# Two-layer attention and expert kernel on one core: window attention of two tiles ahead of the last tile's keys and values, and 120 instead of 40 expert gathers carried from layer 0 into layer 1

## The chip, the cores and the metric

The kernel runs on one core of a Trainium2 chip. The metric is the device time of one execution in microseconds (us). A run is the whole program: both layers, from the loading of the inputs to the stored output.

## What is computed

Two layers over 512 latent tokens and 256 context tokens, width 1024, all in float32. The latent tokens are four tiles of 128 tokens (lat 0 to lat 3), the context is two (ctx 0, ctx 1). Cut to what matters:

```
for l in range(2):
    p  = modulate(h, ...) @ w_in                      # queries, keys, values, lat and ctx
    o1 = softmax(q_mla . [kc_mla, k_mla]) v           # every latent query reads all 256 + 512 keys
    o2 = softmax([q_swa . kc_swa, q_swa . k_near, sink]) v   # 256 context keys + tokens within 128
    h  = h + g1 * (concat(o1, o2) @ w_out)
    b  = modulate(h, ...)
    s  = (b @ wq) . sub_keys                          # 8 heads, two halves of 128 keys
    idx, g = the 16 best experts of 16384 per head    # 128 experts per token
    h  = h + g2 * sum_k g[k] * gelu(b . u[idx[k]]) * v[idx[k]]
```

The context gets its attention and expert step in layer 0 alone. The tile numbers matter: the window attention `o2` of lat 0 reads the keys of lat 0 and 1, that of lat 1 those of lat 0 to 2. The all-key attention `o1` of every tile reads the keys of all four.

## The kernel before

The expert step is done in two ways. **Sparse tiles** (in layer 0 ctx 0, ctx 1 and lat 3; in layer 1 lat 0 and lat 1) fetch the rows that were chosen: the generator `experts` (line 742) yields once per gather, 128 gathers of `u` rows and then 128 of `v` rows for each tile. One gather moves 128 rows of 4 KB into one of five `gv` buffers (line 754, issued by POOL), and VectorE (DVE) does a dot product with it (line 758) or adds it to `vacc` (line 768), four gathers later. After a tile's last gather its new `h` is written to memory (lines 771 to 775). **Dense tiles** (layer 0: lat 0 to 2; layer 1: lat 2 and 3) go through all 16384 experts in `dense_experts` (line 857) as 128 steps: SyncE (SP) loads 512 KB of `uT` and 512 KB of `v`, ScalarE (ACT) and DVE split them into two parts (lines 867, 868), TensorE (PE) multiplies (`A`, line 921; `o`, line 894), and every 16 steps two loads bring the gate weights `G` (line 909).

A layer is first attention and routing, then the dense phase. In the attention part the steps are Python generators run one after the other by `run(...)` or interleaved by `par(...)`: `KV` projects keys and values, `Q` queries, `A` is the attention of one tile (line 524), first the all-key heads, then the window heads, `O` is the output projection, `R` or `RF` routing, `G` and `GH` the choice of the experts and, for a dense tile, the one-hot gate matrices. This gives the order of priority. The instructions themselves are placed by a scheduler that simulates engine times at build time, within dependencies and buffers; each engine then executes its own queue strictly in order. In the dense phase the order is written out by hand (`manual_schedule`).

The gathers of a layer are dealt out in three portions at the end of the layer's code. In layer 0 there are 3 x 256 = 768: 353 (`AHEAD` 0.46) stand ahead of the dense phase, `rest` = 768 - 353 - 40 = 375 are spread over the 128 dense steps, 2.93 to a step, and 40 (`SPILL`) are left over. These 40 are the generator `left`, run in layer 1 after `Q(t, 0)`. They belong to lat 3, whose `h` is complete only behind them, so the keys and values of lat 3 in layer 1 come after them. In layer 1 there are 512: 368 ahead of its dense phase, 144 spread over it from step 16 on. Line 1076 holds the order at the start of layer 1:

```python
run(KV(c, 0, 1), KV(t, 0, 1), Q(t, 0), left, KV(t, 2, 3), A(t, 0), O((t, 0)))
run(RF(t, 0), Q(t, 1), A(t, 1))
run(G(t, 0), O((t, 1)), Q(t, 2, 3))
```

The weights of each projection pass through four `w4` buffers on SP's queue, and three buffers (`fm_tile`) hold the transposed inputs and the attention outputs.

Of the kernel before, what the change touches and what calls it, by code (L numbers as in the profile page):

```python
# [64 lines left out]

LATE = (0, 16)

SPILL = (40, 0)

AHEAD = (0.46, 0.72)  # L70

# [18 lines left out]
def body(ctx: ExitStack, tc: tile.TileContext, I, out):  # L90
# [275 lines left out]
    def fm_tile(name):  # L366
        return att.tile([P, KC, P], F32, tag="aT", name=name, bufs=3)
# [143 lines left out]
    def over_sums(o, su):  # L511


        rs = sm.tile([P, H], F32, tag="rsu", name="rsu")
        nc.vector.reciprocal(rs, su)
        pr = m1()
        for c in range(H // 2):
            for x in range(2):
                nc.tensor.matmul(pr[x * VD:(x + 1) * VD, c * P:(c + 1) * P],
                                 rs[:, 2 * c + x:2 * c + x + 1].to_broadcast([P, VD]), ident, start=True, stop=True)  # L520
        ov = o.rearrange("p c t -> p (c t)")
        nc.vector.tensor_tensor(ov, ov, pr, OP.mult)

    def attend(l, st, i, qT, sqT, K, kv):

        nk = C if st == "ctx" else C + S
        oT = fm_tile("oT")
        su = sm.tile([P, H], F32, tag="su", name="su")
        for c in range(H // 2):
            yield  # L530
            pe = []
            for h in (2 * c, 2 * c + 1):
                ps = big()
                for k0 in range(0, nk, 512):
                    n = min(512, nk - k0)
                    nc.tensor.matmul(ps[:, k0:k0 + n], qT[:, h, :], kv["kT"][:, h, k0:k0 + n],  # L536
                                     start=True, stop=True)
                pe.append(soft(ps, nk, su[:, h:h + 1], None))
            pair_pv(pe, nk, lambda x, kt: kv["v"][:, kt, (2 * c + x) * VD:(2 * c + x + 1) * VD],
                    oT[:, c, :])  # L540
        over_sums(oT[:, 0:4, :], su)
        su = sm.tile([P, H], F32, tag="su", name="su")
        j0, j1 = (0, 0) if st == "ctx" else (max(0, i - 1), min(NT[st], i + 2))
        nk2 = C + (j1 - j0) * P
        for c in range(H // 2):
            yield
            g = c // 2
            pe = []
            for x in range(2):
                hp = x * SD  # L550
                q = sqT[hp:hp + SD, c, :]
                ps = big()
                nc.tensor.matmul(ps[:, :C], q, kv["skT"][hp:hp + SD, g, :C], start=True, stop=True)
                for j in range(j0, j1):
                    dst = ps[:, C + (j - j0) * P:C + (j - j0 + 1) * P]
                    nc.tensor.matmul(dst, q, kv["skT"][hp:hp + SD, g, C + j * P:C + (j + 1) * P],
                                     start=True, stop=(j == i))
                    if j != i:
                        nc.tensor.matmul(dst, identb, mlo if j < i else mhi, start=False, stop=True)
                h = 2 * c + x  # L560
                pe.append(soft(ps, nk2, su[:, h:h + 1], K["nsink"][:, h:h + 1]))
            pair_pv(pe, nk2, lambda x, kt: kv["sv"][:, kt if kt < 2 else kt + j0, g * SD:(g + 1) * SD],
                    oT[:, 4 + c, :])
        over_sums(oT[:, 4:8, :], su)
        return oT

    def out_proj(l, tiles, oT, m):

# [410 lines left out]
    def run(*gens):  # L979
        for g in gens:  # L980
            for _ in g:
                pass
# [11 lines left out]
    for l in range(L):  # L994
# [3 lines left out]
        with ExitStack() as es:  # L998
# [4 lines left out]
            K = layer_consts(l)  # L1003
            kv = {"kT": att.tile([QK, H, C + S], F32, tag="kT", name="kT"),
                  "v": att.tile([P, (C + S) // P, H * VD], F32, tag="v", name="v"),
                  "skT": att.tile([P, 2, C + S], F32, tag="skT", name="skT"),
                  "sv": att.tile([P, (C + S) // P, 2 * SD], F32, tag="sv", name="sv")}
            qs, os, bs = {}, {}, {}

            def KV(st, *tiles):  # L1010
                aT = norms(l, st, tiles, m, st == "lat")
                yield
                yield from project_kv(l, st, tiles, aT, K, kv)

            def Q(st, *tiles):
                aT = norms(l, st, tiles, m, False)
                yield
                yield from project_q(l, st, tiles, aT, K, qs)

            def KVQ(st, *tiles):  # L1020
# [2 lines left out]
                yield from project_kv(l, st, tiles, aT, K, kv)  # L1023
                yield from project_q(l, st, tiles, aT, K, qs)

            def A(st, i):
                os[st, i] = yield from attend(l, st, i, *qs.pop((st, i)), K, kv)

            def O(*tiles):
                res = yield from out_proj(l, tiles, [os.pop(x) for x in tiles], m)  # L1030
                bs.update(zip(tiles, res))
# [7 lines left out]
            def RF(st, i):  # L1039

                bT, bd = bs.pop((st, i))
                half = chosen("")

                def mid(res):
                    yield from choose(*res[0], *half, 0, H // 2)

                r, = yield from route(l, [bT], mid)
                got[st, i] = r, bd, half
# [8 lines left out]
            c, t = "ctx", "lat"  # L1057
            if l == 0:
                a = ada(l, m)
                next(a)  # L1060
                run(KVQ(c, 0, 1))
                run(a, A(c, 0), O((c, 0)))
                early = qs[c, 1][1][:, 0, 0:1]
                par((A(c, 1), 16), (R((c, 0)), 16))
                run(G(c, 0), ada(1, mods[1], early))
                run(KV(t, 0, 1), KV(t, 2, 3), Q(t, 0, 1), A(t, 0), O((c, 1), (t, 0)))
                par((A(t, 1), 8), (R((c, 1), (t, 0)), 24))
                run(G(c, 1), O((t, 1)), Q(t, 2, 3))
                par((A(t, 2), 8), (R((t, 1)), 24), (GH(0), 48))
                run(O((t, 2)))  # L1070
                par((A(t, 3), 8), (R((t, 2)), 24), (GH(1), 48))
                run(O((t, 3)))
                par((R((t, 3)), 24), (GH(2, True), 48))
                run(G(t, 3))
            else:
                run(KV(c, 0, 1), KV(t, 0, 1), Q(t, 0), left, KV(t, 2, 3), A(t, 0), O((t, 0)))
                run(RF(t, 0), Q(t, 1), A(t, 1))
                run(G(t, 0), O((t, 1)), Q(t, 2, 3))
                par((A(t, 2), 8), (R((t, 1)), 24))
                run(G(t, 1), O((t, 2)))  # L1080
                par((A(t, 3), 8), (R((t, 2)), 24))
                run(O((t, 3)))
                par((R((t, 3)), 24), (GH(2), 48))
                run(GH(3, True))
        with ExitStack() as es:
# [9 lines left out]
            free[0] = False  # L1095
            rest = n - int(n * AHEAD[l]) - SPILL[l]
            for e, _ in enumerate(dense):
# [4 lines left out]
            left = rows  # L1102
# [57 lines left out]
```

## Time and profile before

| | us |
|---|---|
| time, median of 3 runs | 4489.13 (4487.55 to 4492.19) |
| the profiled execution, its own time | 4481.78 |
| its span from first to last instruction | 4480.0 |
| PE busy | 3617.1 (81%) |
| DVE busy | 3352.5 (75%) |
| ACT busy | 1687.4 (38%) |
| POOL busy | 1629.0 (36%) |
| mean granted TensorE clock | 0.894 of full speed |

The profiled execution lies 7.35 us below the median. Its stages, by the first and last matmuls of each: attention and routing of layer 0 to 1401 us, dense phase of layer 0 from there to 2517 us, attention and routing of layer 1 to 3640 us, dense phase of layer 1 to the end. All times inside a run are microseconds from the start of the span.

### The profile page before, as it was taken

Reading aid. Unit: us, or ns where it says so; the run is one execution under the profiler, and the core shown is the slowest. Engines: PE = TensorE matmul, PEld = TensorE weight load, DVE = VectorE, ACT = ScalarE, POOL = GpSimd, SP = SyncE. Lnnn points to the kernel's source line nnn. Section 1 sums busy time; section 2 is a strip of 40 time slices with the busy share of each in tenths; the row PEclk is TensorE's granted clock in tenths of the full one; section 3 lists DMA queues with packets and bytes.
Section 4 is the critical chain, followed back from the end, with each engine's and each line's share of the span. In section 5 each row is a group of like instructions: output and inputs, shape, how many; then the busy total and the mean of one; then the engine's idle time right before and its main releaser. Section 6 shows DMA issues by size and latency. Waiting matters only on the chain.

```text
span 4480.0 us, 58044 instructions
## 1 busy us (share of the span) xinstructions
PE 3617.1 (81%) x19934; PEld 2907.9 (65%) x19934; DVE 3352.5 (75%) x7566; ACT 1687.4 (38%) x3244; POOL 1629.0 (36%) x1402
## 2 busy tenths in 40 slices
PE   6885778477887999999999668676676468999997
PEld 2453357256776898888988545444455467888886
DVE  1247778989678788777877832778989977777777
ACT  1342231155575333333333234232224653444443
POOL 2016565544101444444444510255443443222222
PEclk8997788788997999999999889898888579999999
DMA  8588898888666999999999952789899789889897
GB/s 303 171 284 305 307 346 310 299 300 311 219 204 229 327 318 315 325 334 328 332 311 318 330 175 92 258 320 336 310 335 345 260 307 337 301 298 304 298 316 245
DMA packets 467481, 1306.48 MB, mean 292 GB/s; under 512 B 41568, under 2 KB 147808, under 8 KB 467184
## 3 DMA queue, kind: packets, MB, share of 16 engines
q0 software_dynamic: 199744, 726.26, 46.0%
q1 hardware_dynamic: 267440, 576.50, 37.0%
q8 instruction: 157, 2.57, 0.2%
q14 instruction: 140, 1.15, 0.1%
HBM read 1240.70 MB, written 61.90 MB: 291 GB/s over the span
## 4 chain that ended last, share of the span: by engine, by line
PE 24%; issue 24%; DVE 23%; DMA 13%; ACT 8%; POOL 7%; SPq 0%; POOLq 0%; ACTq 0%; DVEq 0%
DVE vacc L768 8%; POOL gv L754 7%; PE m L644 5%; DVE v L868 4%; ACT u L867 3%; DMA gv<-v,idx 3%; DVE gv L758 2%; DMA gv<-u,idx 2%; PE m L372 2%; DMA raw<-uT 2%; PE acc L852 2%; PE A L921 2%; DMA w<-w_in 2%; PE o L894 2%; PE m L507 1%
## 5 line engine op out<-in xcount | busy, mean ns | idle before, releaser
L754 POOL DMA_INDIRECT gv<-v,idx x640 | 782.1, 1222 | 1143.4 <-DVE vacc L768 807.3
L754 POOL DMA_INDIRECT gv<-u,idx x640 | 784.6, 1226 | 964.3 <-DVE a L758 635.4
L894 PE MATMUL o<-v,W 128*128 128x512 f32 x3840 | 943.0, 398 | 71.3 <-ACT W L867 71.0
L921 PE MATMUL A<-b,u 128*128 128x384 f32 (+1 forms) x6144 | 962.5, 313 | 41.6 <-ACT w L924 29.8
L921 PEld LDWEIGHTS A<-b,u 128*128 128x128 f32 x6144 | 936.3, 192 | 70.8 <-ACT w L924 39.3
L894 PEld LDWEIGHTS o<-v,W 128*128 128x128 f32 x3840 | 719.0, 191 | 228.9 <-ACT W L867 84.6
L768 DVE SCALAR_TENSOR_TENSOR vacc<-gv,a,vacc 128x1024 f32<-128x1024 f32 x635 | 811.2, 1277 | 55.7 <-DMA gv<-v,idx 48.5
L758 DVE CUSTOM_DVE_ANT_0 gv<-gv,btok 128x1024 f32<-128x1024 f32 x640 | 768.0, 1218 | 98.0 <-DMA gv<-u,idx 97.1
L867 ACT ACTIVATE W<-w 128x384 fp32r<-128x384 f32 (+1 forms) x256 | 120.7, 472 | 1042.5 <-DVE w L927 1042.5
L868 DVE TENSOR_TENSOR u<-raw,u 128x1024 fp32r<-128x1024 f32 x256 | 313.5, 1224 | 166.3 <-ACT u L867 164.1
L372 PE MATMUL m<-w,aT 128*128 128x256 f32 (+3 forms) x704 | 259.7, 518 | 86.7 <-DMA w<-w_in 51.4
L644 PE MATMUL m<-bT,wq 128*128 128x128 f32 x2560 | 313.7, 279 | 5.0 <-DMA wq<-wq 4.1
L868 DVE TENSOR_TENSOR v<-raw,v 128x1024 fp32r<-128x1024 f32 x256 | 311.9, 1218 | 3.6 <-ACT v L867 3.5
L644 PEld LDWEIGHTS m<-bT,wq 128*128 128x128 f32 x2560 | 301.1, 195 | 10.7 <-DMA wq<-wq 5.7
L867 ACT ACTIVATE u<-raw 128x1024 fp32r<-128x1024 f32 x256 | 267.7, 1046 | 62.5 <-DMA raw<-uT 62.5
L867 ACT ACTIVATE v<-raw 128x1024 fp32r<-128x1024 f32 x256 | 267.4, 1044 | 4.6 <-PE o L894 4.5
L372 PEld LDWEIGHTS m<-w,aT 128*128 128x128 f32 x704 | 142.7, 213 | 190.5 <-DMA w<-w_in 69.2
L868 DVE TENSOR_TENSOR W<-w,W 128x384 fp32r<-128x384 f32 (+1 forms) x256 | 125.7, 491 | 144.7 <-ACT W L867 144.6
L927 DVE TENSOR_TENSOR w<-w,G 128x192 f32<-128x192 f32 (+1 forms) x512 | 143.6, 319 | 68.4 <-DMA G<-Gd 55.2
L852 PE MATMUL acc<-o,o 128*128 128x128 f32 x768 | 140.0, 337 | 66.8 <-ACT ar L853 60.0
L504 ACT ACTIVATE peT<-m 128x512 f32<-128x512 f32 (+1 forms) x192 | 109.5, 576 | 220.0 <-PE m L507 114.3
L536 PE MATMUL big<-kT,qT 96*128 96x256 f32 (+1 forms) x288 | 132.2, 593 | 71.9 <-ACT pexp L484 36.0
(215 smaller groups left out, 4286.0 us busy)
## 6 DMA issues: line engine op xcount, KB each, us to landing
raw<-uT SPq DMA_DIRECT2D x256, 512.0 KB, 5.6
raw<-v SPq DMA_DIRECT2D x256, 512.0 KB, 5.4
wq<-wq SPq DMA_DIRECT2D x144, 512.0 KB, 6.8
gv<-ada_w POOLq DMA_DIRECT2D x80, 512.0 KB, 6.7
Gd<-ar SPq DMA_DIRECT2D x80, 512.0 KB, 4.3
w<-w_out SPq DMA_DIRECT2D x72, 512.0 KB, 6.6
G<-Gd SPq DMA_DIRECT2D x16, 1536.0 KB, 12.4
G<-Gd SPq DMA_DIRECT2D x16, 1024.0 KB, 9.8
```

The source lines that it names most:

```text
L372: nc.tensor.matmul(ps[:, :cn], aT[:, k, :], w[k][:, :cn], start=(k == 0), stop=(k == KC - 1))
L536: nc.tensor.matmul(ps[:, k0:k0 + n], qT[:, h, :], kv["kT"][:, h, k0:k0 + n], start=True, stop=True)
L644: nc.tensor.matmul(ps[:, c], w[:, k, :], bT[:, k, :], start=(k == 0), stop=(k == KC - 1))
L754: return t, nc.gpsimd.indirect_dma_start(out=t, out_offset=None, in_=src, in_offset=bass.IndirectOffsetOnAxis(ap=idx[:, k:k + 1], axis=0))
L758: ins = nc.vector.tensor_tensor_reduce(out=t, in0=t, in1=bt, scale=1.0, scalar=0.0, op0=OP.mult, op1=OP.add, accum_out=a[:, k:k + 1])
L768: return nc.vector.scalar_tensor_tensor(acc, t, w[:, k:k + 1], acc, op0=OP.mult, op1=OP.add)
L852: nc.tensor.matmul(ps[:, x * NK:(x + 1) * NK], o1[:, x], o2, start=True, stop=True)
L867: nc.scalar.activation(hi, x, AF.Copy)
L868: nc.vector.tensor_tensor(lo, x, hi.bitcast(F32), OP.subtract)
L894: nc.tensor.matmul(acc[t][x], W[:, a_, c], v[:, b_, x * 512:(x + 1) * 512], start=(e == 0 and (a_, b_) == PARTS[0]), stop=(e == NK - 1 and ...
L921: nc.tensor.matmul(A, u[:, a_, k * P:(k + 1) * P], b[:, b_, k], start=(k == 0 and (a_, b_) == PARTS[0]), stop=(k == KC - 1 and (a_, b_) == ...
L927: nc.vector.tensor_tensor(wv[:, x], wv[:, x], gc[x][:, :, e % GC, :], OP.mult)
```

## The change

Three things change. `SPILL[0]` goes from 40 to 120: 80 more gathers of lat 3 leave the dense phase of layer 0 (`rest` becomes 295, or 2.30 to a step) and are run in layer 1. `attend` is split in two functions, one for the all-key heads and one for the window heads, with the output tile allocated outside. And the order at the start of layer 1 is rewritten: the keys and values of lat 2 are projected by themselves ahead of the leftover gathers, the queries of lat 0 and lat 1 together; the window attention of lat 0 and lat 1 (`AN`) follows the gathers in priority, then the keys and values of lat 3, then the all-key attention (`AA`) of lat 0. What is left of lat 1's attention after the routing of lat 0 is its all-key part.

```diff
-SPILL = (40, 0)
+SPILL = (120, 0)
...
-    def attend(l, st, i, qT, sqT, K, kv):
+    def attend_all(l, st, i, qT, K, kv, oT):
         nk = C if st == "ctx" else C + S
-        oT = fm_tile("oT")
         su = sm.tile([P, H], F32, tag="su", name="su")
...
         over_sums(oT[:, 0:4, :], su)
+
+    def attend_near(l, st, i, sqT, K, kv, oT):
         su = sm.tile([P, H], F32, tag="su", name="su")
...
         over_sums(oT[:, 4:8, :], su)
-        return oT
...
+            def AN(st, i):
+                os[st, i] = fm_tile("oT")
+                yield from attend_near(l, st, i, qs[st, i][1], K, kv, os[st, i])
+
+            def AA(st, i):
+                yield from attend_all(l, st, i, qs.pop((st, i))[0], K, kv, os[st, i])
+
             def A(st, i):
-                os[st, i] = yield from attend(l, st, i, *qs.pop((st, i)), K, kv)
+                os[st, i] = fm_tile("oT")
+                qT, sqT = qs.pop((st, i))
+                yield from attend_all(l, st, i, qT, K, kv, os[st, i])
+                yield from attend_near(l, st, i, sqT, K, kv, os[st, i])
...
-                run(KV(c, 0, 1), KV(t, 0, 1), Q(t, 0), left, KV(t, 2, 3), A(t, 0), O((t, 0)))
-                run(RF(t, 0), Q(t, 1), A(t, 1))
+                run(KV(c, 0, 1), KV(t, 0, 1), KV(t, 2), Q(t, 0, 1), left, AN(t, 0), AN(t, 1), KV(t, 3), AA(t, 0), O((t, 0)))
+                run(RF(t, 0), AA(t, 1))
```

## Rows read from the trace of the kernel before

**Rows 1.** The page's second part, the span in 40 slices of 112 us: busy tenths of PE, and of the DMA engines.
```profile
PE   6885778477887999999999668676676468999997
...
DMA  8588898888666999999999952789899789889897
```

**Rows 2.** The order of time on PE in the dense phase of layer 0, around a load of the gate weights: start, duration, engine, line, operation, count, and in brackets the idle time ahead of it with what ended that.
```profile
1665.22 4.35 PE L921 MATMUL A<-b,u 128*128 128x384 f32 x24
...
1673.53 4.35 PE L921 MATMUL A<-b,u 128*128 128x384 f32 x24
...
1688.48 5.99 PE L894 MATMUL o<-v,W 128*128 128x512 f32 x18 [2.30 <-ACT W L867]
```

**Rows 3.** The group of line 921 in the dense phase of layer 0: shortest, median and longest duration in ns, first and last start in us.
```profile
L921 PE MATMUL A<-b,u x3072: 333/334/688, 1401.2 to 2504.1; 128*128 128x384 f32 x192
```

**Rows 4.** What PE waited for between 1400 and 2517 us: total us, times, longest.
```profile
PE o L894 <- ACT W L867: 19.4, 12, 2.8
PE A L921 <- ACT w L924: 16.6, 10, 2.7
```

**Rows 5.** The page's sixth part, loads of the gate weights: count, size of one, median us from issue to landing. The first is layer 0's, the second layer 1's.
```profile
G<-Gd SPq DMA_DIRECT2D x16, 1536.0 KB, 12.4
G<-Gd SPq DMA_DIRECT2D x16, 1024.0 KB, 9.8
```

**Rows 6.** The order of time on POOL from the end of the dense phase of layer 0: the first and the last of the 40 gathers that are left over, and the store of lat 3's new `h`.
```profile
2510.64 1.43 POOL L754 DMA_INDIRECT gv<-v,idx  x1 [0.30 <-issue]
...
2588.93 1.09 POOL L754 DMA_INDIRECT gv<-v,idx  x1 [0.30 <-issue]
...
2600.87 0.54 POOL L775 DMA_DIRECT2D h_lat<-gv  x1 [8.69 <-DVE hss L242]
```

**Rows 7.** The order of time on PE from the end of the dense phase of layer 0 to the output projection of lat 1 in layer 1.
```profile
2510.73 5.95 PE L894 MATMUL o<-v,W 128*128 128x512 f32 x18 [2.21 <-ACT W L867]
2549.73 3.75 PE L265 MATMUL m<-diag,hld 128*128 128x128 f32 x16 [33.04 <-DMA h_lat<-h]
...
2610.77 3.28 PE L265 MATMUL m<-diag,hld 128*128 128x128 f32 x16
...
2655.31 5.40 PE L372 MATMUL m<-w,aT 128*128 128x384 f32 x16 [0.52 <-DVE q L417]
...
2734.05 5.49 PE L536 MATMUL big<-kT,qT 96*128 96x512 f32 x8 [2.98 <-ACT pexp L484]
...
2781.29 1.04 PE L507 MATMUL m<-peT,sv 128*64 128x128 f32 x16
...
2810.41 9.19 PE L644 MATMUL m<-bT,wq 128*128 128x128 f32 x80
...
2854.54 2.04 PE L619 MATMUL m<-keys,pq 128*128 128x128 f32 x8 [11.26 <-issue]
...
2896.47 2.85 PE L536 MATMUL big<-kT,qT 96*128 96x512 f32 x8 [0.34 <-ACT qT L363]
...
2936.43 1.04 PE L519 MATMUL m<-ident,rsu 128*64 128x128 f32 x16
...
2968.94 10.45 PE L575 MATMUL big<-w,oT 128*128 128x512 f32 x20 [3.29 <-DVE oT L522]
```

**Rows 8.** The order of time on PE in layer 0, where the same projections and the attention of lat 0 run beside gathers of ctx 0: keys and values of lat 0 and 1 (first row to second), queries of lat 0 and 1 and the attention of lat 0 (third row to fourth).
```profile
382.06 3.75 PE L265 MATMUL m<-diag,hld 128*128 128x128 f32 x16 [0.94 <-DVE diag L255]
...
444.94 0.44 PE L425 MATMUL m<-ident,lowr 128*128 128x128 f32 x2 [1.58 <-DVE lowr L422]
449.86 2.90 PE L372 MATMUL m<-w,aT 128*128 128x384 f32 x4 [4.47 <-DMA w<-w_in]
...
591.12 0.49 PE L519 MATMUL m<-ident,rsu 128*64 128x128 f32 x5
```

**Rows 9.** Gathers of line 754 alone in three stretches: from and to, length, POOL's busy time and the number of gathers, granted clock, DMA share, GB/s. The first is the stretch of rows 8, the second the attention and routing of layer 1, the third lies in the first steps of layer 1's dense phase.
```profile
504.00:640.00 136.00, 84.21 (x68) 0.86 0.92 331
...
2860.00:3640.00 780.00, 366.18 (x321) 0.79 0.88 315
...
3676.00:3749.00 73.00, 41.26 (x32) 0.95 0.98 371
```

**Rows 10.** All engines in four stretches of layer 1: from and to, length, busy us (and instructions) of PE, PEld, DVE, ACT and POOL, granted clock, DMA share, GB/s. Keys and values of the context; those of lat 0 and 1; all from there to the routing of lat 0; that routing.
```profile
2549.00:2610.00 61.00, 40.43 (x138) 27.45 (x138) 42.50 (x61) 20.78 (x59) 27.13 (x23) 0.78 0.86 314
2610.00:2656.00 46.00, 35.79 (x142) 24.80 (x143) 10.44 (x46) 16.97 (x50) 0.00 (x0) 0.89 0.39 126
...
2600.00:2810.00 210.00, 162.74 (x787) 107.90 (x787) 57.80 (x191) 85.05 (x217) 0.54 (x1) 0.89 0.36 116
2810.00:2866.00 56.00, 36.48 (x296) 34.85 (x297) 35.85 (x268) 4.88 (x8) 3.42 (x4) 0.82 0.59 195
```

**Rows 11.** The order of time on PE in the first steps of layer 1's dense phase: its first matmuls, the first matmuls of two steps that lie ten steps apart, and of two neighbouring steps behind them.
```profile
3639.60 5.23 PE L921 MATMUL A<-b,u 128*128 128x256 f32 x24 [1.20 <-ACT ar L853]
...
3676.76 2.90 PE L921 MATMUL A<-b,u 128*128 128x256 f32 x22 [1.08 <-DVE u L868]
...
3748.73 3.92 PE L921 MATMUL A<-b,u 128*128 128x256 f32 x22 [2.64 <-DVE u L868]
...
3755.74 3.04 PE L921 MATMUL A<-b,u 128*128 128x256 f32 x24
...
3761.36 3.04 PE L921 MATMUL A<-b,u 128*128 128x256 f32 x24
```

## Prediction, made before the changed kernel was run

> **What bounds the kernel now.** I read the slices first, then the stage from which work is taken, then the stage to which it goes, and last the stage behind that. In the slices [rows 1] the reader sees two plateaus in which PE is nine tenths busy or more, the two dense phases, and around slice 24 a valley in which the DMA engines fall to five and two tenths. The change carries gathers from the first plateau into that valley, so the question is what each of the two is bound by.
>
> The plateau is PE's. A step starts every 1673.53 - 1665.22 = 8.31 us and no idle time stands ahead of either row [rows 2]. Line 921 starts at 1401.2 us [rows 3] and the last matmul of the phase ends at 2510.73 + 5.95 = 2516.7 [rows 7]: 1115.5 us, against 128 x 8.31 = 1063.7. The phase loses 52 us, of which PE's recorded waits are 19.4 + 16.6 = 36 us [rows 4]; the row behind a gate-weight load shows their form, a short wait and then matmuls at longer durations [rows 2].
>
> The valley is a chain. From 2600 to 2810 us PE is busy for 163 of 210 us, DVE for 58, the DMA engines for 0.36 of the time [rows 10]: projections, attention of lat 0, and its output projection hand on to one another, and only when lat 0 is routed can layer 1's gathers begin. Behind it, in the 780 us of routing, gathers run at 780 / 321 = 2.43 us each with the DMA engines 0.88 busy [rows 9], and layer 1's dense phase starts at 3639.6 [rows 11].
>
> **What the change takes from layer 0's dense phase.** 80 gathers and 80 additions on DVE, none of them on PE's path. PE's 1063.7 us stay. Of the 52 us that are lost anything from 0 to 52 could come back (it can't get longer, since only work leaves). The nearest rows are the gate loads: in layer 1, where fewer than half as many gathers go with each step (144 over 128 against 375), 1024 KB take 9.8 us; in layer 0 1536 KB take 12.4 [rows 5]. That is 104 KB/us against 124: thinner gathers did not make this load faster. So I take **-5 us**, near the lower end.
>
> **What it adds at the start of layer 1.** Pace of the gathers: the 40 left over were issued from 2510.64 to 2588.93 [rows 6], 78.3 us over 39 intervals, 2.0 us each; beside the same projections in layer 0 it was 136 / 68 = 2.0 as well [rows 9]. So 120 take 240 us, from 2506 to 2746, and 12 more from the last issue to the store of lat 3 (2600.87 - 2588.93, [rows 6]): 2758.
>
> What can PE do in that time? The keys and values of the context took 61 us beside gathers, 2549.73 to 2610.77 [rows 7]. Those of lat 0 and 1 took 44.5 us without gathers (to 2655.31), but in layer 0, with gathers beside them, 382.06 to 445.4, or 63.3 us [rows 8]: a factor of 1.42. The reason can be read off DVE: it executes in order, each addition waits for its landing, and the projections' scaling, rope and maxima are queued behind it; PE and ACT wait for those. Queries of lat 0 and 1 and one tile's attention took 449.86 to 591.6 = 142 us there [rows 8]; the two window attentions together are about one tile's attention (16 heads), so I use it for them.
>
> The chain, 5 us early from the dense phase: 2544.7, + 61 = 2605.7, + 63.3 = 2669, + half of 63.3 for lat 2 = 2701. Until 2758 it gets through 57 of the 142 us; the other 85 go without gathers, / 1.42 = 60: 2818. Keys and values of lat 3, half of 44.5, go halfway beside the window attention: + 12. All-key attention of lat 0 is half of 2734.05 to 2782.3 [rows 7]: + 24. From there to routing's first matmul as before, 2810.4 - 2782.3 = 28: **2882, 72 us later than before** (2810.4). Lower end: with no slowing at all (63.3, 32 and 142 all divided by 1.42, 167 instead of 212) it is 2837, +27. Upper end: gathers at layer 1's 2.43 us last to 2810 and everything runs beside them: 2701 + 142 + 12 + 24 + 28 = 2907, +97.
>
> Queues that the moved steps pass: on SP the load of lat 3's `h` waits for its store at 2758, and the weights of lat 3's projection and of lat 0's output projection stand behind it; PE asks for them at 2818, so 60 us cover this. If the gathers ran over by more than that, every us would count. Weights are loaded once more for keys and values (lat 2 and 3 apart), once less for queries (lat 0 and 1 together): no term. The three `fm_tile` buffers hold two attention outputs until lat 1's output projection, which leaves one for `aT` and `bT`; each of these is asked for one at a time: no term.
>
> **What it gives back.** From routing of lat 0 to the output projection of lat 1 it was 2968.9 - 2810.4 = 158.5 us [rows 7], with the queries of lat 1 and its whole attention in it. Now there is routing, to 2856.6, or 46.2 us; the all-key attention, 2896.47 to 2937.5, or 41 us [rows 7]; and 3.3 us of waiting for DVE: 90.5. So **-68 us**. Ends: -88 if half of the 41 us fit into routing, where PE is busy for only 36.5 of 56 us [rows 10]; -40 if the gathers beside them stretch the 90.5 by 1.3.
>
> **What is late next.** Layer 1's dense phase starts when the last routing is done, so at 3640 + 72 - 68 = 3644. But its first gather comes 72 us later, and the stretch for them is 68 us shorter: 68 / 2.43 = 28 fewer are done by then. These run in the first dense steps. There ten steps took 3748.73 - 3676.76 = 72 us, 7.20 each, with 32 gathers beside them [rows 9, 11], where a step without them takes 3761.36 - 3755.74 = 5.62: (72 - 56.2) / 32 = 0.49 us per gather. 28 of them: **+14 us**. Ends: 0, if later steps have room, and 28 x 73 / 32 = 64, if no step ran beside them.
>
> **Sum** against the profiled execution: +72 (with the -5 in it) - 68 + 14 = +18, from 4481.8 to 4500. That execution is 7.35 us under the median; on the median 4489.1 + 18 = **4507**. 9 us, 0.2%, is about what a measurement of this kernel can tell from no change.
>
> **Rivals.**
> *The steps that are moved are covered (faster).* The start is a chain with idle time, and PE, ACT and DVE take the window attention and lat 1's queries in it. Then routing starts midway between my value and the lower end, +50, the all-key attention of lat 1 fits half into routing, -88, and 36 fewer gathers cost 18: -20, **4469**. For it: 163 of 210 us busy on PE, 58 on DVE. Against: layer 0's twin of this stretch, slow by 1.42. It decides the sign as soon as routing of lat 0 starts before 2864 (+54), if the rest is as I sum it.
>
> *The dense phase gives back half of its loss.* If the gate loads do speed up as a fifth of the gathers goes, -26 instead of -5 comes off: **4486**, no change that can be measured. Against it is the pair of load times above. The Trainium skill, "DMA: Bandwidth & Descriptors", section on queues, rings and completion order, says that each DMA engine goes round-robin between the queues that have work, a packet at a time; by that a gate load would gain in every moment in which the gathers' queue is empty, and the sum would be 4486. The rate of the loads in layer 1, 104 against 124 KB/us, does not bear this out.
>
> *The gathers take too long.* At 2.43 us each they end at 2810, +97; less 68, plus 14 to 64: 4532 to 4582, say **4550**. For it: two kinds of transfer beside each other, DMA share already 0.92 [rows 9]; against: the pace of 2.0 in two places.
>
> *The change doesn't do what it says.* The scheduler, not the text, places instructions; if it puts the window attentions behind the keys of lat 3, nothing but the queries covers the gathers. Queries would be done near 2780, then 23 + 24 + 48 + 28: 2903, +93, less 68, plus 14: **4528**.
>
> **How the numbers follow.** Forecast 0.40, its own range 4490 to 4530; covered steps 0.27; dense phase 0.13; slow gathers 0.13; other order 0.07. Faster by over 0.2% (below 4480): 0.25 of the covered case and 0.04 of the dense case, 0.29. Slower (above 4498): 0.31 of the forecast, 0.13, 0.07 and 0.01 of the dense case, 0.52. Same: 0.19. The range goes from 4445, the covered case with more of the dense loss returned, to 4575, slow gathers with most of the backlog unhidden; some 0.08 lies outside on each side.
>
> **What the profile afterwards would show.** Dense phase of layer 0: 1110 us, steps still 8.31. The store of lat 3 near 2758. Routing's first matmul of line 644 near 2882; if it is before 2864, or after 2910, the first term is wrong. From there to line 575 for lat 1 about 90 us. First matmul of layer 1's dense phase near 3644, and steps at 7.2 us for some nine steps more than before. The valley's DMA share should rise from 0.36 to about 0.9. The prediction is wrong if gathers beside projections no longer slow them, if the dense phase of layer 0 shortens by more than 20 us, or if routing behind lat 1 turns out to be bound by DVE and not by the chain, so that the 68 us don't come back.

## The result, and the profile after

The changed kernel takes **4524.56 us** (median of 4 runs, 4523.37 to 4532.22); the kernel before, on the same chip, 4490.66. The ratio is **1.0095 [1.0079, 1.011]**: slower by 34 us. The profiled execution of after is 4532.22 us, 7.7 above its median, and that of before lies under its median, so the two traces differ by 50.4 us where the medians differ by 34. The sum below goes by the traces, with the forecast's terms beside it.

The page's second part of after, PE and the DMA engines in 40 slices:
```profile
PE   7886778487978999999997668858756485999997
...
DMA  8578898888566888888888991498888899889897
```
In slices 23 to 25 (counted from 0) the DMA engines had a five, a two and a seven [rows 1]; they now have a nine, a one and a four: the valley was not filled, it moved behind the gathers that were to fill it. On PE the 8 of slice 33, early in layer 1's dense phase, has become a 5.

The stages, from the first matmuls of each in the two traces (us; the dense phase of layer 0 goes to the end of its last matmul):

| stage | before | after | difference | forecast |
|---|---|---|---|---|
| start of layer 0's dense phase | 1401.2 | 1393.2 | -8 | 0 |
| that phase | 1115.5 | 1071.4 | **-44** | -5 |
| its end to layer 1's first matmul | 33.0 | 33.6 | +1 | 0 |
| from there to routing of lat 0 | 260.7 | 384.7 | **+124** | +77 |
| from there to layer 1's dense phase | 829.2 | 763.8 | **-65** | -68 |
| layer 1's dense phase to the end of the span | 840.4 | 883.8 | **+43** | +14 |
| sum | | | +50 | +18 |

(The first row varies from 1384 to 1407 among runs whose code up to there is the same.) Dense phase of layer 0 in after: the group of line 923 (median duration in ns, first and last start), then what PE waited for from 1390 to 2465 us:
```profile
L923 PE MATMUL A<-b,u x3072: 333/334/686, 1393.2 to 2456.1; 128*128 128x384 f32 x192
```
```profile
PE A L923 <- ACT w L926: 1.9, 1, 1.9
```
Of the two waits of [rows 4], 36 us together, 3 us are left (1.9 in this row, 1.1 for `W`). Next the start of layer 1 on PE, in order of time:
```profile
2498.25 2.05 PE L265 MATMUL m<-diag,hld 128*128 128x128 f32 x8 [33.64 <-DMA h_lat<-h]
...
2563.52 0.85 PE L265 MATMUL m<-diag,hld 128*128 128x128 f32 x3
...
2635.84 2.47 PE L265 MATMUL m<-diag,hld 128*128 128x128 f32 x10 [0.93 <-DVE diag L255]
...
2663.60 2.85 PE L372 MATMUL m<-w,aT 128*128 128x384 f32 x8 [0.69 <-DVE q L417]
...
2735.32 0.70 PE L556 MATMUL big<-skT,sqT 64*128 64x256 f32 x2 [0.69 <-ACT sqT L470]
...
2795.60 2.33 PE L265 MATMUL m<-diag,hld 128*128 128x128 f32 x16
...
2850.60 0.70 PE L577 MATMUL big<-w,oT 128*128 128x512 f32 x1 [1.10 <-DVE oT L522]
...
2882.93 1.27 PE L646 MATMUL m<-bT,wq 128*128 128x128 f32 x9
...
2957.54 1.98 PE L577 MATMUL big<-w,oT 128*128 128x512 f32 x4 [1.15 <-DVE oT L522]
```
Read as a chain: keys and values of the context 65 us, of lat 0 and 1 72, of lat 2 28, both queries 72, both window attentions 60, keys and values of lat 3 with the all-key attention of lat 0 55, output projection 32, then routing. POOL (which issues the gathers) in the same stretch, the last left-over gather, lat 3's store, and the next instruction:
```profile
2700.74 0.94 POOL L756 DMA_INDIRECT gv<-v,idx  x1 [4.40 <-DVE vacc L770]
...
2711.73 0.54 POOL L777 DMA_DIRECT2D h_lat<-gv  x1 [6.13 <-DVE gv L776]
2886.66 0.53 POOL L786 DMA_DIRECT2D btok<-b_lat  x1 [174.39 <-DMA b_lat<-hld]
```
Lat 3's new `h` is on its way to memory at 2711.7; its keys begin at 2795.6, behind the window attentions. POOL then stands idle for 174 us. Last, layer 1's dense phase: one place in the order of time on PE, and its largest wait in the whole phase (total, times, longest):
```profile
3757.03 3.04 PE L923 MATMUL A<-b,u 128*128 128x256 f32 x24
...
3770.09 3.03 PE L923 MATMUL A<-b,u 128*128 128x256 f32 x24
3825.87 5.49 PE L896 MATMUL o<-v,W 128*128 128x512 f32 x12 [52.75 <-ACT W L869]
3831.16 3.19 PE L923 MATMUL A<-b,u 128*128 128x256 f32 x24
```
```profile
PE o L896 <- ACT W L869: 97.9, 35, 52.7
```
One step takes 61.1 us (3770.09 to 3831.16). The same step took 14.4 before:
```profile
3766.98 3.03 PE L921 MATMUL A<-b,u 128*128 128x256 f32 x24
3781.40 3.04 PE L921 MATMUL A<-b,u 128*128 128x256 f32 x24
```
The steps around it have the same lengths in both traces, mostly 5.6 to 6.4. So the 43 us of this stage are one wait. In the long step of after DVE does 31 dot products of late gathers one behind the other (3770.4 to 3824.9 us), busy for 38 of 55 us and otherwise waiting for landings; only then does it come to the `w` that ACT's `W` needs.

### The profile page after: what moved, and what is told of

Its sections match the earlier page's. It is cut to its first block, busy times and chain, and to the rows that moved or that the text cites. A ratio compares the mean times of both kernels' runs of the same rounds, so it can differ in the third digit from the quotient of the medians.

```text
span 4530.5 us, 58055 instructions
## 1 busy us (share of the span) xinstructions
PE 3640.1 (80%) x19934; PEld 2928.9 (65%) x19934; DVE 3358.0 (74%) x7566; ACT 1700.7 (38%) x3243; POOL 1650.7 (36%) x1402
## 4 chain that ended last, share of the span: by engine, by line
PE 42%; DVE 20%; issue 13%; DMA 13%; ACT 7%; POOL 4%; SPq 0%; ACTq 0%; POOLq 0%; DVEq 0%
PE o L896 11%; PE A L923 11%; DVE vacc L770 5%; PE m L646 5%; POOL gv L756 4%; DMA gv<-v,idx 3%; DVE gv L760 3%; DMA gv<-u,idx 3%; DVE v L870 3%; ACT u L869 2%; PE m L372 2%; DMA raw<-uT 2%; PE m L500 2%; PE m L507 2%; PE acc L854 1%
## 5 line engine op out<-in xcount | busy, mean ns | idle before, releaser
L756 POOL DMA_INDIRECT gv<-v,idx x640 | 796.0, 1244 | 1171.8 <-DVE vacc L770 797.2
L926 ACT ACTIVATE w<-A 128x384 f32<-128x384 f32 (+1 forms) x256 | 109.3, 427 | 299.2 <-PE A L923 299.2
L480 DVE TENSOR_REDUCE nb<-big 128x1 f32<-128x768 f32 (+3 forms) x160 | 122.4, 767 | 111.4 <-PE big L535 55.7
```

The source lines that it names most:

```text
L480: nc.vector.tensor_reduce(nb, ps[:, :n], AX.X, OP.max, negate=True)
L756: return t, nc.gpsimd.indirect_dma_start(out=t, out_offset=None, in_=src, in_offset=bass.IndirectOffsetOnAxis(ap=idx[:, k:k + 1], axis=0))
```

## Experiments

The theory after this reading: (a) layer 0's dense phase was late because DVE, not PE or a load, had no time to spare in a step; (b) the start of layer 1 pays for the work that was moved into it, since on a chain nothing covers it, and for 80 gathers more; (c) what routing gives back is that same work; (d) the gathers that are late hold up layer 1's dense phase. Rivals: the left-over gathers alone make the loss and the order is a gain; the gate loads in the DMA engines set layer 0's phase; every late gather costs its time wherever it stands.

### The two parts of the change apart

**e1_spill_old_order**: the kernel before with only the first hunk.
```
-SPILL = (40, 0)
+SPILL = (120, 0)
```


> The order of before with 120 gathers left over: the spill alone. Theory 1 (the dense phase of layer 0 gains because VectorE gets slack, and the new order is not what costs): dense phase of layer 0 at 1071 us instead of 1115; routing of lat 0 begins earlier than the 2883 of the changed kernel, near 2840, but lat 1's queries and whole attention come behind it (158 us instead of 75), so layer 1's dense phase starts near 3680, with a block of gathers at its step 16 of 50 us or more: 4540 to 4570 us. Rival (the rewritten order is what costs the 35 us): below 4500 us.

**e2_order_only**: the kernel after with only the order.
```
-SPILL = (120, 0)
+SPILL = (40, 0)
```


> The new order with 40 gathers left over: the order alone. Theory 1: the dense phase of layer 0 stays at 1115 us; at the start of layer 1 the projections run without gathers from about 2600 on, routing of lat 0 begins near 2850 and lat 1's output projection near 2930, 40 us earlier than before; but layer 1's gathers start 40 us later, so 45 us come back as a block at step 16 of its dense phase: 4480 to 4505 us. Rival (the order is a loss by itself): above 4510 us.

Measured: e1 4514.1 us, ratio 1.0063 [1.0046, 1.0081]; e2 4524.88, ratio 1.0085 [1.0058, 1.0112]. Both parts lose, and the order loses as much as the whole change. The time of e1 lies between the ranges of its two theories; that of e2 is the rival's, where I had expected no clear loss. By stages, against before:

| | dense 0 | start of layer 1 | routing stretch | dense 1 |
|---|---|---|---|---|
| e1, 80 gathers more | -46 | +77 | +2 | -4 |
| e2, order | -1 | +66 | -65 | +41 |
| after, both | -44 | +124 | -65 | +43 |

The busy times tell why the order gains nothing. All engines from layer 1's first matmul to routing of lat 0, and from there to the dense phase (from and to, length, busy us and instructions of PE, PEld, DVE, ACT, POOL, granted clock, DMA share, GB/s), in the kernel before:
```profile
2549.70:2810.40 260.70, 196.23 (x898) 130.24 (x898) 95.84 (x236) 102.15 (x266) 27.13 (x23) 0.87 0.47 160
2810.40:3639.60 829.20, 542.59 (x3184) 411.47 (x3183) 708.08 (x2104) 316.70 (x664) 369.13 (x327) 0.80 0.86 308
```
the same two in e2:
```profile
2553.90:2881.00 327.10, 258.32 (x1201) 169.73 (x1201) 118.40 (x291) 134.27 (x336) 27.34 (x23) 0.88 0.41 137
2881.00:3645.40 764.40, 486.49 (x2882) 380.26 (x2880) 650.95 (x1985) 281.06 (x593) 326.21 (x295) 0.78 0.86 306
```
the first of them in e1:
```profile
2509.30:2846.80 337.50, 211.32 (x899) 138.40 (x900) 193.38 (x316) 103.01 (x266) 126.24 (x103) 0.80 0.69 249
```
and both in after:
```profile
2498.20:2882.90 384.70, 287.80 (x1200) 184.74 (x1200) 214.75 (x371) 135.66 (x336) 130.12 (x103) 0.79 0.63 226
2882.90:3646.70 763.80, 492.87 (x2882) 385.65 (x2880) 649.77 (x1984) 281.44 (x593) 338.62 (x294) 0.76 0.86 306
```
In e2, 303 matmuls more came into the start, 258.32 - 196.23 = 62 us of PE, and the stretch grew by 66; PE's idle time stayed at 260.7 - 196.2 = 64 against 69. The routing stretch lost 302 matmuls, 56 us of PE, and 65 us. The work was moved and paid at its full length on both sides. With the gathers PE is idle for 126 us in e1 and for 97 in after, so the moved work does cover 29 us of the gathers' cost, at the price of 287.80 - 211.32 = 76 us of PE. What stays is that the stretch in which layer 1 gathers is 65 us shorter: 289 gathers fit into it instead of 321, and the 32 others are in the dense phase.

### The gathers at the start of layer 1

**e9_left_dve_half** and **e10_left_dma_half**: the kernel after, where additions (e9) or transfers (e10) of left-over gathers are half as wide; `l < cur[0]` holds for a gather of layer 0 that is emitted in layer 1.
```
 def add(k, t, w, acc, half):
+    if half:
+        t, acc = t[:, :D // 2], acc[:, :D // 2]
...
+    row(partial(add, k, t, a, acc, l < cur[0]), ins)
```


> The kernel after; the additions of the gathers left over from layer 0 are made on 512 of their 1024 columns when they are emitted beside layer 1's start (half of each is left out); the gathers fetch whole rows. If these gathers cost 0.96 us each because their additions stand in DVE's queue ahead of the projections' scaling and rope, 120 x 0.6 = 72 us less DVE work brings routing of lat 0 to 325 to 355 us from the start of layer 1 (384.7 after the change) and the whole to 4470 to 4500. If DVE waits for landings whatever an addition costs, or the projections wait for their own weights beside the gathers, routing stays at 375 to 390 us and the whole at 4515 to 4530.


```
+if l < cur[0]:
+    return t, nc.gpsimd.indirect_dma_start(out=t[:, :D // 2], ..., in_=src.rearrange("e (x d) -> (e x) d", x=2), ...)
...
+return nc.vector.scalar_tensor_tensor(both(acc, half), twice(t, half), w[:, k:k + 1], both(acc, half), ...)
```


> The kernel after; the gathers left over from layer 0, when they are issued beside layer 1's start, fetch only half of their row (512 of 1024 columns; the other half of the expert's row is left out of the addition), while their additions take DVE as long as before. Halving the additions alone took 20 us from the way to routing of lat 0 (384.7 to 364.3). If the rest of the slowing lies in the DMA engines, where these gathers stand beside the projections' weights at a share of 0.9 or more, half the bytes bring routing to 330 to 355 us from the start of layer 1 and the whole to 4480 to 4505. If the slowing is only the work that was moved, routing stays at 370 to 388 us and the whole at 4515 to 4530.

Measured, one run each: e9 4520.01, routing at +364.3; e10 4516.06, routing at +375.1 (after: +384.7). The first lies between the two values of its expectation, the second in the range for "no effect of bytes". How far such numbers can be trusted is told by three runs further on (e3, e11, e13) that have the order and the left-over gathers of after: 377.5, 380.1 and 375.5 us. So the 10 us of e10 are inside the spread of this stretch, and no effect of the bytes is shown; the additions are worth 11 to 20 us of the 384.7 - 327.1 = 58 that 80 gathers cost here. What the rest hangs on is in part PE's clock (last section) and otherwise open.

### Layer 0's dense phase

**e4_dve_half** and **e5_dma_half**: the kernel before, with DVE's part of a gather halved at full transfers, and the other way round.
```
 def dot(k, t, bt, a, g):
+    c = slice(0, D if free[0] or l else D // 2)
+    ins = nc.vector.tensor_tensor_reduce(out=t[:, c], in0=t[:, c], in1=bt[:, c], ...)
...
 def add(k, t, w, acc):
+    c = slice(0, D if free[0] or l else D // 2)
+    return nc.vector.scalar_tensor_tensor(acc[:, c], t[:, c], w[:, k:k + 1], acc[:, c], ...)
```


> The kernel before, but in the dense phase of layer 0 the dot products and additions of the gathers work on 512 of the 1024 columns (half of each is left out); every gather still moves its 512 KB. Theory 1 (VectorE has no slack of its own at 2.93 gathers to a step, so each late gate load goes through to PE): with 1.8 us of VectorE time less per step the waits of PE in that phase fall from 36 us to under 10 and the phase from 1115 to some 1071 us. Rival (fewer bytes beside the gate loads are what helped): the phase stays near 1115 us, since the bytes are the same.

In e5 an addition reads the half row twice, and a dot product is made of two instructions over the same half (both left out here):
```
+if not free[0] and not l:
+    return t, nc.gpsimd.indirect_dma_start(out=t[:, :D // 2], ..., in_=src.rearrange("e (x d) -> (e x) d", x=2), ...)
```


> The kernel before; while layer 0's dense phase runs, each gather fetches only half of its row (512 of 1024 columns, so the other half of the expert's row is left out of the dot product and of the addition), and DVE does the same number of columns as before. If the steps are late because DVE has no lead over PE (8.33 us of work in a step of 8.31), nothing changes: the dense phase stays at 1110 to 1116 us and PE's two waits behind ACT at 30 to 37 us. If they are late because the gathers hold up the gate loads in the DMA engines, the loads fall from 12.4 us to 9 or less, the dense phase to 1070 to 1090, and the whole to 4435 to 4455.

Measured, one run each: e4 4437.44 with a phase of 1086.8 us (before 1115.5); e5 4476.56 with 1111.4. What PE waited for in that phase of e5:
```profile
PE o L909 <- ACT W L882: 14.9, 11, 2.5
PE A L936 <- ACT w L939: 11.2, 6, 3.8
```
Half the bytes leave 26 of the 36 us of waits and 1111.4 of 1115.5; half of DVE's work takes 29 us off. But e5 did not leave DVE's work as it was: two half dot products take 2 x 0.69 us where one whole takes 1.22, and DVE was busy for 928 us in the phase instead of 905. The fair comparison is by the 71 steps that hold additions almost alone (13 to 55 and 99 to 126, counted from 0). At PE's pace of 8.31 they would take 590 us; they took 620.7 in before, 608.1 in e5 and 596.4 in e4. Half of DVE's work gives back 24 of the 31 us lost there, half the bytes 13. So DVE comes first, and the bytes count too. In e4 15 of the 44 us that the change took off did not come back, though an addition there takes 0.75 us instead of 1.28: DVE waits 46 us for gate loads (before 27), and the two longest steps, of 13.2 us each, stand where such a wait is longest (8.2 and 8.3 us).

By the order of time on DVE one sees what it lacks. A step of the kernel before (bracket: idle time ahead of the row and what ended it):
```profile
1801.12 1.22 DVE L868 TENSOR_TENSOR u<-raw,u 128x1024 fp32r<-128x1024 f32 x1 [0.39 <-ACT u L867]
1802.26 1.22 DVE L868 TENSOR_TENSOR v<-raw,v 128x1024 fp32r<-128x1024 f32 x1
1803.40 3.92 DVE L768 SCALAR_TENSOR_TENSOR vacc<-gv,a,vacc 128x1024 f32<-128x1024 f32 x3
1807.24 0.62 DVE L927 TENSOR_TENSOR w<-w,G 128x192 f32<-128x192 f32 x2
1808.51 0.56 DVE L868 TENSOR_TENSOR W<-w,W 128x384 fp32r<-128x384 f32 x1 [0.65 <-ACT W L867]
1809.46 1.22 DVE L868 TENSOR_TENSOR u<-raw,u 128x1024 fp32r<-128x1024 f32 x1 [0.40 <-ACT u L867]
```
From `u` to `u` 8.34 us: DVE's own loop, with three additions and two waits for ACT that come in every step, is as long as PE's step of 8.31. A late gate load is then made up only in the 9 of 128 steps that have two. This shows only in DVE's rows, since PE's own list names ACT. In after a step has two or three additions or dot products (2.3 on average), and one with two needs 1.3 us less. (By PE's pace and the 12.5 us of the last step in after, a phase without any loss would take 127 x 8.31 + 12.5 = 1068 us, so the 1071.4 of after gave back nearly all that there was.)

### Filling the wait

If the loop is what counts, a wait in it can be used. **e7_fill**: the kernel before, with one addition of each step between the multiplications by the gate and the low half of `W`.
```
     nc.vector.tensor_tensor(wv[:, x], wv[:, x], gc[x][:, :, e % GC, :], OP.mult)
+yield
...
-for e, _ in enumerate(dense):
-    for _ in range(<count of step e>):
+for z, _ in enumerate(dense):
+    e = z // 2
+    cnt = <count of step e>
+    for _ in range(min(1, cnt) if z % 2 else cnt - min(1, cnt)):
         next(rows, None)
```


> The kernel before with one thing moved: of the additions (or dot products) of a dense step on DVE, one stands between the multiplications by the gate and the low half of W, where DVE waits 0.65 us for ACT's high half in every step. Same gathers, same bytes, same arithmetic. If DVE's closed loop is what sets the steps, a step's DVE time falls by up to 0.65 us, so that 3 additions go in under 7.8 us: layer 0's dense phase 1070 to 1090 us (before 1115), layer 1's 815 to 830 (before 840), in all 4420 to 4450. If PE's waits come from the gate loads, the dense phases stay within 8 us and the time within 10 us of before; and since the addition now stands ahead of W's low half, on which PE waits, it can also cost up to 0.6 us a step: 4490 to 4560.

Measured: **4388.16 us, ratio 0.9796 [0.9769, 0.9822]**. That is less than either range of the expectation. Layer 0's phase is 1078.8 us, inside its range. Layer 1's is 779.6 (before 840.4), where 815 to 830 was expected: 31 of its steps from the 20th on have two dot products or additions, and their median falls from 6.43 to 5.62 us, that of the steps with one. By their means (6.57 and 5.69) this is 27 of the 61 us; the rest was not taken apart. A step of DVE and PE's waits in layer 0's phase:
```profile
1649.16 1.23 DVE L868 TENSOR_TENSOR u<-raw,u 128x1024 fp32r<-128x1024 f32 x1
1651.58 1.23 DVE L868 TENSOR_TENSOR v<-raw,v 128x1024 fp32r<-128x1024 f32 x1 [1.20 <-ACT v L867]
1652.72 2.60 DVE L768 SCALAR_TENSOR_TENSOR vacc<-gv,a,vacc 128x1024 f32<-128x1024 f32 x2
1655.24 0.62 DVE L927 TENSOR_TENSOR w<-w,G 128x192 f32<-128x192 f32 x2
1655.78 1.28 DVE L768 SCALAR_TENSOR_TENSOR vacc<-gv,a,vacc 128x1024 f32<-128x1024 f32 x1
1656.97 0.55 DVE L868 TENSOR_TENSOR W<-w,W 128x384 fp32r<-128x384 f32 x1
```
```profile
PE A L921 <- ACT w L924: 5.6, 4, 2.3
PE o L894 <- ACT W L867: 2.6, 2, 1.5
```
The waits of 0.65 and 0.39 us are gone; what is left, 1.20 us ahead of `v`, is DVE's lead: it waits for an ACT that keeps PE's pace. ACT's own rows, in before and in e7, show the turn: first it waited for DVE, now for PE.
```profile
1807.95 0.53 ACT L867 ACTIVATE W<-w 128x384 fp32r<-128x384 f32 x1 [5.54 <-DVE w L927]
```
```profile
1658.79 1.06 ACT L867 ACTIVATE v<-raw 128x1024 fp32r<-128x1024 f32 x1 [1.36 <-PE o L894]
```
That the gate loads alone set the phase is answered by DVE's waits for them in layer 0's phase, again in before and in e7. They got longer, and yet the phase got shorter:
```profile
DVE w L927 <- DMA G<-Gd: 26.9, 7, 4.5
```
```profile
DVE w L927 <- DMA G<-Gd: 35.2, 8, 7.8
```

**e8_fill_spill0** is e7 without left-over gathers (`SPILL = (0, 0)`), and **e12_fill_two** is e8 with a second such place, between the low halves of `W` and of `u`:
```
     down(e - 1, Ws[e - 1], vs[e - 1])
+yield
```


> The same move of one addition, and no gathers left over from layer 0 (before 40, after the change 120). At 0.96 us for each gather left over, as the run with 120 of them in the old order showed, the start of layer 1 is 38 us shorter. If the filled wait leaves DVE enough lead, the 40 more gathers in layer 0's dense phase cost little (0 to 15 us): 4395 to 4430. If DVE is again without a lead at 3.3 additions a step, they cost 1.3 us each, 52 us: 4440 to 4475, no better than the move alone.

> The kernel before with no gathers left over and two additions moved: one between the multiplications by the gate and the low half of W (a wait of 0.65 us), one between the low half of W and that of u (0.39 us). With one move and nothing left over layer 0's dense phase took 1106 us and the whole 4391. If DVE's second wait is what is left, the phase falls to 1070 to 1090 and the whole to 4355 to 4375. If the gate loads or PE set the phase by now, or the additions ahead of u's low half hold up PE, it stays at 1100 to 1115 and 4380 to 4400.

Measured: e8 4390.98, ratio 0.9791 [0.9769, 0.9813], layer 0's phase 1106.8; e12 **4381.87, ratio 0.9767 [0.9741, 0.9794]**, layer 0's phase 1089.8, the lowest time of all runs, though 7 us above its expectation and by its interval not apart from e7 or e8. In e8 the start was 12 us shorter than in e7 and the pause ahead of layer 1's first matmul 18 us shorter (2497.9 to 2515.8, in e7 2468.4 to 2504.3), 30 where 38 were expected, and layer 0's phase took back 28 of them: with one filled wait DVE has no lead over 3.2 additions a step.

### The late gathers in layer 1's dense phase

**e3_ahead65**: the kernel after, with fewer of layer 1's gathers ordered ahead of the dense steps.
```
-AHEAD = (0.46, 0.72)
+AHEAD = (0.46, 0.65)
```


> The changed kernel with 332 instead of 368 gathers of layer 1 ahead of its dense phase and 180 instead of 144 spread over steps 16 to 127 (1.61 to a step). Theory 1 (some 30 gathers that are not done in time run as one block in front of step 16, PE idle for 52.7 us): the block goes, the later steps have the room (VectorE 3.3 + 1.6 x 1.22 = 5.3 of 5.6 us), 4470 to 4485 us, less than before. Rival (the gathers cost their time wherever they stand): the steps behind 16 stretch and it stays at 4510 to 4525 us.

Measured: 4515.3, ratio 1.0074 [1.005, 1.0098]. The step of 61.1 us is 9.0, but the other steps with two additions stretch to 6.3 to 6.8, and the phase is 876.3 instead of 883.8. This looked like the rival: a gather costs its time wherever it stands. With DVE's wait filled it could be asked again: **e11_after_fill** is after with e7's edit, **e13_after_fill_ahead65** that with e3's.

> The kernel after, with one addition of each dense step moved into DVE's wait behind the multiplications by the gate, as in the run that did so to the kernel before (4388.2 us). If the price of the change is the same once DVE has a lead in both dense phases, layer 0's phase is 10 us shorter than in that run (no more than 1068), layer 1's start +124, the give-back -65, and the backlog in layer 1's dense phase costs 0.49 us a gather or less, since DVE no longer sets its steps: +0 to +16 instead of +41, in all 4425 to 4460, slower than the fill alone by 0.9 to 1.6%. If the change only lost to the backlog, it would now be faster than the fill alone: under 4380.

> The kernel after with one addition of each dense step moved into DVE's wait, and 332 instead of 368 of layer 1's gathers ahead of the dense steps. The run with the move alone took 4478.8 us, with one step of 60.4 us in layer 1's dense phase (before the change 14.4), in which steps wait until the gathers that are ordered ahead of step 17 are done. If the change's backlog costs through this order alone, the long step falls to 10 to 20 us, the others stay near 5.6 because DVE now has a lead, layer 1's dense phase falls from 838 to 785 to 800, and the whole to 4420 to 4440. If each gather that is left for the dense steps costs its time wherever it stands, as without the move (876 against 884 us), the phase stays at 825 to 840 and the whole at 4460 to 4485. Above 4400 in both cases, because the start of layer 1 is still 117 us longer than in the run that moved one addition in the kernel before, and gives back 73.

Measured: e11 4478.79, ratio 0.9984 [0.997, 0.9999], outside what either theory gave, with layer 1's phase at 838.3 and one step of 60.4 us; e13 **4432.87, ratio 0.9893 [0.9856, 0.9929]**, that phase at 795.6, both in the range for a cost through the order alone. The same place in the order of time on PE in e13:
```profile
3748.89 3.04 PE L923 MATMUL A<-b,u 128*128 128x256 f32 x24
...
3754.51 3.03 PE L923 MATMUL A<-b,u 128*128 128x256 f32 x24
...
3762.66 3.13 PE L923 MATMUL A<-b,u 128*128 128x256 f32 x24 [0.81 <-ACT w L926]
...
3768.82 3.04 PE L923 MATMUL A<-b,u 128*128 128x256 f32 x24
```
With 368 gathers ordered ahead the backlog costs one long step, whether DVE has a lead (60.4 us in e11) or not (61.1 in after). With 332 it costs through DVE when DVE has no lead (e3, where the median step is 6.55 us) and little when it has one (e13, 5.62). And the change, with this cost mostly gone, still loses 4432.87 - 4388.16 = 45 us against e7: layer 0's phase -9, start +112, routing stretch -75, layer 1's phase +16, together +44.

## Why the prediction was right, and where its terms were off

The forecast of 4507 us, slower, had the sign and half of the loss; 4524.56 lies in its own range of 4490 to 4530. The mechanism, a start that pays for more than routing gives back and a backlog behind it, was right. Of its four terms one was right and three mis-sized, by 39 us one way and by 47 and 29 the other. That the sum came as near as it did is partly luck. By the prediction's own signs the part on layer 0's dense phase was wrong (it shortened by more than 20 us), and so were three of its forecasts for the profile: the store of lat 3 came at 2711.7 and not near 2758 (its stage began 46 us earlier), the DMA share from 2600 to 2810 us is 0.58 and not about 0.9 (it is 0.91 up to 2712, while gathers run), and the backlog is one step and not some nine longer ones.

**Layer 0's dense phase, -5: it gave 44.** The step that failed is the choice of the nearest row: I looked at the rate of the gate loads [rows 5], found no gain with thinner gathers (191 of them, not 144, ran in layer 1's dense phase), and took the lower end. The loads alone were not what decided. Where PE's time was lost, the row behind a gate load [rows 2] names ACT; the question to ask was why the step could not catch up, and DVE's loop of 8.34 us answers it. The rival "gives back half" was nearer in size (-26), by a mechanism that is the smaller part: faster loads. The Trainium skill's page that stood beside that rival ("DMA: Bandwidth & Descriptors", section on queues, rings and completion order) has each DMA engine go round between the queues that have work; the trace agrees so far that with half the bytes beside them the gate loads land in 10.6 us instead of 12.4. Faster loads do not decide the phase: in e7 they take 13.3 us and the phase is 33 us shorter than in e5. (Loads of the gate weights in e5 and in e7:)
```profile
G<-Gd SPq DMA_DIRECT2D x16, 1536.0 KB, 10.6
```
```profile
G<-Gd SPq DMA_DIRECT2D x16, 1536.0 KB, 13.3
```
**Start of layer 1, +77 counted from its first matmul: it was +124.** Routing came at 2882.9, where 2882 was forecast, but from a start that lay 46 us ahead of the one I had reckoned with: two errors that hid each other. The gathers went as forecast (2.0 us each; the store 213.5 us after layer 1's first matmul, forecast 213.3), and so did the keys and values (65 + 72 + 28 = 165 us, forecast 156). (Of the two sources for 2.0, the stretch of 136 us begins behind layer 0's keys and values; beside them, from 382 to 445 us, it was 33 gathers in 63 us, 1.9 each, so the figure holds.) What was wrong is the rest, 72 + 60 + 55 = 187 us to the output projection, where I had 57 + 60 + 12 + 24 = 153. I divided layer 0's 142 us for queries and attention by 1.42 for the part without gathers. That factor was measured on keys and values. Window attention ran without any gather, and still took 60 us, because PE itself is busy in it:
```profile
2735.00:2796.00 61.00, 55.38 (x391) 42.51 (x392) 22.07 (x63) 34.82 (x87) 0.00 (x0) 0.83 0.02 6
```
(All engines of after in that stretch.) What was left to gain is idle time, and here there is 6 us of 61. In part the +124 is also this one trace: e3, e11 and e13, with the same order and gathers, have +115 to +119.

**Give-back, -68: -65.** Right in sum. To the output projection of lat 1 it was 74.6 us instead of the forecast 90.5, a gain of 84, of which 19 were lost again before the dense phase. DVE is busy for 0.85 of the whole routing stretch in both kernels, and gathers run at the same DMA share of 0.86; which of them takes the 19 was not tried.

**Backlog, +14: +43.** The number, 28 gathers, was near (32 fewer before the phase, by e2). The price of 0.49 us was read from ten early steps in which PE is late anyway [rows 9, 11]. Those steps did not get longer (the first 16 took 115.9 us, before 121.8); the gathers pile up ahead of one step, at 47 / 32 = 1.5 us each. The upper end of this term, 64, held it.

**The rivals.** Covered steps: refuted by e2, where the order alone costs what it moves; beside the gathers 29 of 76 us were covered. Dense phase: see above. Slow gathers: refuted, their pace was 2.0. Other order: refuted, window attention starts at 2735.3 and lat 3's keys at 2795.6.

## What to carry to other kernels

Work that was moved to an earlier place on the same chain was paid there at PE's full busy time; before such work counts as cover, ask how much of that stretch PE is idle, and what waits behind it. Where two engines have loops of nearly equal length, look for the small waits that come in every step on the in-order engine that is not named by the other's waits: one addition put into such a wait was worth 2% here, while moving gathers and steps to other stages lost 0.6 to 1%. A count of operations that are ordered ahead of a step is a wait for all of them, and it must be set again when the stretch before it changes.

## What was not expected of the hardware

The same 1200 or 1201 matmuls of layer 1's start took 258 us of PE at a granted clock of 0.88 (e2) and 288 at 0.79 (after), when 80 more gathers ran beside them and PE stood idle for 97 us instead of 69: of the 58 us that these gathers cost there, half is PE's own time at a lower clock, not waiting. Busy time times clock is the same in both, 227 us. The size varies between runs with the same gathers (283 us at 0.80 in e3, 276 at 0.83 in e13), so the 275 us at 0.84 of the run with half-wide additions show no effect of the additions on the clock. Which of the idle pauses lowered the clock was not tried.
